# A fast-matrix-product encoder layer: first units of the second feed-forward product into the freed `h` buffers, gate rows three steps ahead of their dots

## The chip, the cores and the metric

The kernel runs on one core of one Trainium2 chip. The metric is the time of one launch on the device in microseconds, lower is better. Three runs of the kernel before gave 1226.02, 1227.35 and 1228.89 us, median 1227.35 us. All traces are from that single core.

## The reference, cut to what matters

One layer of a hybrid encoder: a token-mixing part (gated MLP beside windowed attention) and then a SwiGLU feed-forward part, each scaled by vectors that are computed from a condition `c`. Only the end of it is touched by the change:

```python
mod = jax.nn.silu(c) @ w_ada + b_ada
sh1, sc1, gt1, sh2, sc2, gt2 = jnp.split(mod[:, None, :], N_MOD, axis=-1)
...
h2 = rmsnorm(x, norm2_g) * (1.0 + sc2) + sh2
f_gate, f_up = jnp.split(h2 @ w_ffn_in, 2, axis=-1)
x = x + gt2 * ((jax.nn.silu(f_gate) * f_up) @ w_ffn_out)
```

There are 1024 tokens and 1024 channels, the hidden width is 2816, and all of it is float32. `gt2`, the gate vector, has 1024 entries, and each is the dot of `silu(c)` with a column of `w_ada`. The kernel holds everything transposed: channels on the 128 partitions, tokens along a row.

## The kernel before, in words

**Numbers.** Each float32 operand is split into a high part (a cast on ScalarE, ACT) and a low part (source minus high part, on VectorE, DVE). A product is then three matmuls of TensorE (PE): high by high, high by low, low by high. `wh`/`wl` and `oh`/`ol` are the high and low parts of weights or units; `raw` is what was loaded.

**The first product** (`h2 @ w_ffn_in`) runs over 22 tiles `f` of 128 hidden channels. A tile is done by a seven-product scheme in place of eight, so it has seven steps `i` = 0 to 6 (`STEPS`, L1512), each of 12 matmuls of 128x512. The blocks `B11` and `B21`, read by steps 0 and 1 alone, stand in the four buffers of the pool `hpool` with the tag `h`. For the tiles 2 to 5 steps 0 and 1 are done earlier, so these tiles have five steps here. After the step's `product(f, i)` comes `evict(f, i)`, which reads the bank of PSUM that the product wrote; step 6 accumulates into the bank that `evict(f, 4)` reads, so its matmuls wait for that read (`xs<-mm` on DVE).

**The hidden tiles** go to DRAM as they are finished (`hR`, and `hT` for the last two). The second product takes them as 4 by 2 blocks and `w_ffn_out` as 4 by 4 blocks and forms the block product by 26 products in place of 32 (the list `ORDER`, with eight more that are the plain tail of the last two hidden tiles). Each of the 26 products needs a linear combination of weight blocks (`a` values) and one of hidden blocks (`b` values). These combinations are made on DVE during the first product: the table `SUMS` gives for a step number s (counted from tile 2, step 2) which additions are done and which blocks are loaded, and into which of fifteen registers. A register is a 128x512 piece of a tile: registers 0 to 3 lie in one `sums` tile, 4 is `ss`, 5 and 6 are `t`, 7 to 10 are the other `sums` tile, `gt2["m"]`, and 11 to 14 are `hid`. A combination that a product needs is stored to the DRAM tensor `pU` by POOL's queue (`pool_dma`, L1396); loads go through SP's queue (`dma`, L1399), which issues in order and stops at the first transfer whose buffer isn't free.

**The gate vector.** `gt2_step(n)` (L2142) multiplies row n-1 of `w_ada` by the condition and sums it (the dot, `sums<-sums 128x1024` on DVE, in `ada_late`, L744), then issues the load of row n into the same half of `gt2["m"]`. The rows and the condition share the space of registers 7 to 10, which `SUMS` therefore uses only after the last dot.

**The second product** works on units: product p, group g of 128 in the contraction, a 128x768 float32 piece of `pU` (384 KB): 256 columns of an `a` value and 512 of a `b` value. A unit takes six matmuls. `fetch(n)` loads unit n, `split_step(n)` splits it, `after_unit(n)`, called after the matmuls of unit n, splits unit n+5 and fetches a later one. Units 0 to 2 are fetched during the last tile into `wpool`; the next ones, 3 to 11, after `ffn_ctx.close()`, into the pool `outp`, which lies in the space that the first product's `ffn` pool gives back. `load_acc` brings the residual rows (`mid<-x1d`, 512 KB each, eight of them, on POOL's queue), and `evict_out` adds a finished product to them. `tail_load` and `tail_split` bring and split the operands of the plain tail, whose split tiles also stand in `hpool`.

The order of the instructions on each engine is the order of the calls in the code.

Of the kernel before, what the change touches and what calls it, by code (L numbers as in the profile page):

```python
# [16 lines left out]
P = 128  # L17
# [223 lines left out]
def kernel(  # L241
# [1999 lines left out]
    raws, ready = {}, {}  # L2241
    outp = []

    def fetch(n):
        if n < len(work):
            p, g = work[n]
            if outp:
# [302 lines left out]
```

## Time and profile before

| | before |
|---|---|
| median of three runs | 1227.35 us |
| the profiled execution | 1226.68 us |
| span of that execution | 1224.9 us |
| mean granted TensorE clock | 0.995 |
| PE busy | 1201.7 us, 98% of the span |
| DVE busy | 1009.5 us, 82% |
| ACT busy | 610.3 us, 50% |
| mean rate of the DMA engines | 233 GB/s |

The profile is of one execution. A row of the timeline reads: start in us from the span's start, busy us, engine, line, operation, `out<-in`, shape, count, and in brackets the idle time just before with what ended it. A row of the chain of waits reads: start, us, what. A row of the busy times by stretch gives the stretch, its length and then busy time and count for PE, PEld (weight loads), DVE, ACT and POOL, the granted clock, the share of time that the DMA engines were busy, and GB/s. Between the span and the time of the execution lie 1.8 us.

### The profile page before, as it was taken

To read this page: it belongs to the slowest core of one execution; us is meant where nothing else is said; L and a number is where in the kernel's file an instruction comes from. 1 tells how busy PE (TensorE), PEld (TensorE's weight loads), DVE (VectorE), ACT (ScalarE), POOL (GpSimd) and SP (SyncE) were. 2 spreads that over 40 slices of the span, in tenths; PEclk is the share of its full clock that TensorE was granted. 3 is DMA by queue.
4 is the path that set the end of the run, shared out by engine and by line. 5 is a ranking of instruction groups with operands and counts; after the bars stand their busy time and mean duration, and the time that the engine had idled before them with its cause. 6 is when DMAs were issued, how large, how long until landed. Compare 5 with 4: busy or idle time off the path is not lost.

```text
span 1224.9 us, 16517 instructions
## 1 busy us (share of the span) xinstructions
PE 1201.7 (98%) x5593; PEld 997.6 (81%) x5593; DVE 1009.5 (82%) x1660; ACT 610.3 (50%) x1007; POOL 247.0 (20%) x342
## 2 busy tenths in 40 slices
PE   9999999999999999999997899999999998999998
PEld 7888888888888888888886688888888886788887
DVE  9999967889888876999876788888877866987895
ACT  6668844367856344736552233333333234754562
POOL 0124322104331100012001234333323322000001
PEclk9999999999999999999998999999999999999999
DMA  9745179653286633576227889888876749987884
GB/s 369 279 155 189 35 255 325 255 213 121 80 305 235 225 125 113 168 262 220 90 86 253 289 287 312 316 279 292 271 240 230 267 155 377 379 292 222 295 295 145
DMA packets 108166, 284.87 MB, mean 233 GB/s; under 512 B 13680, under 2 KB 24688, under 8 KB 107056
## 3 DMA queue, kind: packets, MB, share of 16 engines
q1 hardware_dynamic: 84576, 204.36, 49.6%
q0 software_dynamic: 23504, 79.45, 16.8%
q8 instruction: 44, 0.72, 0.2%
q14 instruction: 42, 0.34, 0.1%
HBM read 207.47 MB, written 76.28 MB: 232 GB/s over the span
## 4 chain that ended last, share of the span: by engine, by line
PE 82%; DVE 7%; DMA 6%; issue 2%; ACT 1%; POOL 0%; SPq 0%; DVEq 0%; ACTq 0%; POOLq 0%
PE mm L279 45%; PE at L279 37%; DMA raw<-pU 3%; DMA sums<-in_w_ada_dram 2%; DVE mid L279 1%; DVE wl L279 1%; DVE ws L279 1%; DMA raw<-in_w_tail_dram 1%; DVE sums L279 1%; ACT wh L279 1%; DVE hid L279 1%; DMA pU<-ss 1%; DVE lb L279 1%; DMA mid<-in_xA_dram 0%; DVE xs L279 0%
## 5 line engine op out<-in xcount | busy, mean ns | idle before, releaser
L279 PE MATMUL mm<-mid,wh 128*128 128x512 f32 x640 | 200.8, 395 | 11.0 <-DVE xs L279 10.5
L279 ACT CAST wh<-raw 128x1024 fp32r<-128x1024 f32 (+2 forms) x164 | 155.3, 949 | 86.5 <-PE mm L279 39.1
L279 DVE TENSOR_TENSOR wl<-raw,wh 128x1024 fp32r<-128x1024 f32 (+2 forms) x151 | 161.5, 1077 | 39.4 <-ACT wh L279 38.5
L279 PEld LDWEIGHTS mm<-mid,wh 128*128 128x128 f32 x640 | 121.3, 191 | 37.7 <-DVE xs L279 11.3
L279 PE MATMUL mm<-mid,wl 128*128 128x512 f32 x320 | 126.4, 395 | 0.1
L279 PE MATMUL mm<-wh,h 128*128 128x512 f32 x384 | 124.7, 397 | 0.2 <-ACT h L279 0.2
L279 PE MATMUL mm<-h,wh 128*128 128x512 f32 x304 | 94.4, 392 | 0.0
L279 PE MATMUL at<-h,wh 128*128 128x512 f32 x304 | 94.0, 391 | 0.0
L279 ACT CAST wh<-ws 128x1024 fp32r<-128x1024 f32 (+1 forms) x50 | 48.3, 966 | 76.5 <-DVE ws L279 75.1
L279 ACT CAST oh<-raw 128x768 fp32r<-128x768 f32 x73 | 60.8, 839 | 47.6 <-PE mm L279 20.8
L279 PEld LDWEIGHTS mm<-wh,h 128*128 128x128 f32 x384 | 70.8, 188 | 13.8 <-ACT h L279 0.4
L279 DVE TENSOR_TENSOR ol<-raw,oh 128x768 fp32r<-128x768 f32 x73 | 67.9, 953 | 15.4 <-ACT oh L279 15.1
L1397 POOL DMA_DIRECT2D pU<-sums x84 | 50.9, 607 | 111.0 <-DVE sums L279 104.7
L279 PEld LDWEIGHTS mm<-mid,wl 128*128 128x128 f32 x320 | 60.9, 190 | 13.8 <-DVE wl L279 1.0
L279 PE MATMUL mm<-wl,h 128*128 128x512 f32 x192 | 71.3, 392 | 0.0
L279 DVE TENSOR_TENSOR wl<-ws,wh 128x1024 fp32r<-128x1024 f32 (+1 forms) x50 | 55.9, 1118 | 15.8 <-ACT wh L279 15.7
L279 PEld LDWEIGHTS at<-h,wh 128*128 128x128 f32 x304 | 57.2, 189 | 11.8
L279 ACT ACTIVATE xs<-xs 128x512 f32<-128x512 f32 x21 | 13.3, 633 | 106.3 <-DVE xs L279 106.3
L279 PEld LDWEIGHTS mm<-h,wh 128*128 128x128 f32 x304 | 56.7, 188 | 11.6
L279 ACT ACTIVATE t<-t 128x512 f32<-128x512 f32 x46 | 28.4, 630 | 71.1 <-DVE t L279 71.1
L279 PE MATMUL mm<-h,wl 128*128 128x512 f32 x152 | 59.3, 390 | 0.0
L279 PE MATMUL at<-h,wl 128*128 128x512 f32 x152 | 59.3, 390 | 0.0
(360 smaller groups left out, 2999.7 us busy)
## 6 DMA issues: line engine op xcount, KB each, us to landing
raw<-pU SPq DMA_DIRECT2D x80, 384.0 KB, 5.0
pU<-sums POOLq DMA_DIRECT2D x71, 256.0 KB, 4.7
mid<-in_w_ada_dram SPq DMA_DIRECT2D x30, 512.0 KB, 8.1
raw<-in_w_gate_dram SPq DMA_DIRECT2D x26, 512.0 KB, 4.4
raw<-hR SPq DMA_DIRECT2D x40, 256.0 KB, 4.1
pU<-hid POOLq DMA_DIRECT2D x34, 256.0 KB, 4.3
raw<-in_w_ab_dram SPq DMA_DIRECT2D x16, 512.0 KB, 5.7
pd<-t POOLq DMA_DIRECT2D x24, 256.0 KB, 4.6
```

The source lines that it names most:

```text
L279: ins = f(*args, **kw)
L1397: nc.gpsimd.dma_start(dst, src)
```

## The change

Four things are altered, and all of them lie in the time from the first product's tile 2 to the start of the second product.

1. `gt2_step` runs at every third step (s = 0, 3, ... 24) in place of every second (s = 0, 2, ... 16).
2. The table `SUMS` is another one: the same 174 additions and 156 stores, with 113 loads in place of 106, in another order and with other registers. Registers 7 to 10 are used from s = 27 on; before it was from s = 18.
3. Units 3 to 9 are fetched during steps 2 to 5 of the last tile into `hpool`'s four `h` buffers, two units to a buffer. After `ffn_ctx.close()` units 10 to 18 are fetched in place of 3 to 11, and `after_unit(n)` fetches unit n+14, from n = 5 on, in place of n+12.
4. The tail operands and the residual rows are loaded at later units (`TAIL_AT`, `ACC_AT`).

```diff
 SUMS = (
-    (1, (), (('a', 0, 0, 0), ('a', 0, 4, 1))), (2, (), (('a', 0, 12, 2),)), (3, (), (('a', 0, 2, 3),)),
-    (4, (('a', 0, 16, 4, 0, 1, 1, -1),), ()), (5, (('a', 0, 25, 2, 1, 2, -1, -1),), (('a', 0, 10, 0),)),
-    (6, (('a', 0, 17, 4, 4, 3, 1, -1),), ()), (7, (('a', 0, 18, 1, 4, 1, 1, 1),), (('a', 0, 11, 2),)),
+    (1, (), (('a', 0, 4, 0), ('a', 0, 12, 1))), (2, (), (('a', 0, 0, 2),)), (3, (), (('a', 0, 2, 3),)),
+    (4, (('a', 0, 25, 4, 0, 1, -1, -1),), ()), (5, (('a', 0, 16, 2, 2, 0, 1, -1),), (('a', 0, 10, 1),)),
+    (6, (('a', 0, 17, 4, 2, 3, 1, -1),), ()), (7, (('a', 0, 18, 0, 4, 0, 1, 1),), (('a', 0, 11, 2),)),
...
+    first_raws = []
+
     def fetch(n):
         if n < len(work):
             p, g = work[n]
             if outp:
                 r = outp[0].tile([P, UCOL], F32, tag="raw2", name=nm("raw2"))
+            elif n < 3:
+                r = wpool.tile([P, UNIT], F32, tag="raw", name=nm("raw"))[:, :UCOL]
             else:
-                r = wpool.tile([P, UNIT], F32, tag="raw", name=nm("raw"))[:, :UCOL]
+                if n % 2:
+                    first_raws.append(hpool.tile([P, 2048], F32, tag="h", name=nm("first")))
+                r = first_raws[-1][:, (n + 1) % 2 * UNIT : (n + 1) % 2 * UNIT + UCOL]
...
     acc = {}
-    TAIL_AT = (11, 14, 17, 20)
-    ACC_AT = {4: 7, 8: 0, 14: 6, 18: 1, 24: 3, 45: 2}
+    FIRST_RAWS = 10
+    TAIL_AT = (18, 20, 22, 24)
+    ACC_AT = {13: 7, 17: 0, 23: 6, 27: 1, 31: 3, 55: 2}
...
-                if s < 18 and s % 2 == 0:
-                    gt2_step(s // 2)
+                if s < 27 and s % 3 == 0:
+                    gt2_step(s // 3)
                 run_sums(s)
+            if f == NF - 1 and 2 <= i < 6:
+                for n in (2 * i - 1, 2 * i):
+                    if n < FIRST_RAWS:
+                        fetch(n)
...
-        for n in range(3, 12):
+        for n in range(FIRST_RAWS, FIRST_RAWS + 9):
             fetch(n)
...
             split_step(n + AHEAD_OF)
-            fetch(n + 12)
+            if n + AHEAD_OF + 9 >= FIRST_RAWS + 9:
+                fetch(n + AHEAD_OF + 9)
```

An entry of `SUMS` is (s, additions, loads). An addition is (kind, group or pair of groups, value, register written, two registers read, two signs); a load is (kind, group, value, register).

DVE around the first two dots, from tile 2's step 5 on. `sums_6249,acc_mod` is the dot, `xs_6242<-at` is `evict(2, 5)`, `hid` is `evict(2, 6)`, `ss_6251` is register 4, and the names in brackets are the semaphores waited for (DMAHW for loads, DMASW for stores by POOL). Before:

```order
L279 SCALAR_TENSOR_TENSOR sums_6249,acc_mod<-sums_6249 128x1024 [waits DMAHW7_49,DMAHW0_49]
L279 TENSOR_TENSOR xs_6242<-at_6254,xs_6242 128x512 [waits PE_49]
L279 TENSOR_TENSOR ws_5754<-raw_6161,ru 128x512 [waits DVE_49]
L279 TENSOR_TENSOR ws_5754<-raw_6161,ws_5754 128x512
L279 SCALAR_TENSOR_TENSOR hid_6063<-xs_6267,xs_6242 128x512 [waits DMASW4_49,Activation_49]
L279 SCALAR_TENSOR_TENSOR hid_6063<-mm_5854,t_1093_5870 128x512 [waits DMASW3_49,PE_49]
L279 TENSOR_TENSOR wl_6323<-ws_5754,wh_6322 128x1024 [waits Activation_49]
L279 SCALAR_TENSOR_TENSOR sums_6249,acc_mod<-sums_6249 128x1024 [waits DMAHW3_49]
L279 TENSOR_TENSOR ss_6251<-sums_6250 128x512 [waits DMAHW2_49,DMAHW1_49]
L279 TENSOR_TENSOR wl_6351<-ru,wh_6350 128x512 [waits Activation_49]
L279 SCALAR_TENSOR_TENSOR sums_6250<-sums_6250 128x512 [waits DMAHW4_49]
L279 SCALAR_TENSOR_TENSOR sums_6249,acc_mod<-sums_6249 128x1024 [waits DMAHW7_49]
```

And now:

```order
L283 TENSOR_TENSOR xs_6242<-at_6254,xs_6242 128x512 [waits PE_49]
L283 SCALAR_TENSOR_TENSOR sums_6249,acc_mod<-sums_6249 128x1024 [waits DMAHW7_49,DMAHW0_49]
L283 TENSOR_TENSOR ws_5754<-raw_6161,ru 128x512 [waits DVE_49]
L283 TENSOR_TENSOR ws_5754<-raw_6161,ws_5754 128x512
L283 SCALAR_TENSOR_TENSOR hid_6063<-xs_6267,xs_6242 128x512 [waits DMASW4_49,Activation_49]
L283 SCALAR_TENSOR_TENSOR hid_6063<-mm_5854,t_1093_5870 128x512 [waits DMASW3_49,PE_49]
L283 TENSOR_TENSOR wl_6323<-ws_5754,wh_6322 128x1024 [waits Activation_49]
L283 SCALAR_TENSOR_TENSOR ss_6251<-sums_6250 128x512 [waits DMAHW2_49,DMAHW1_49]
L283 TENSOR_TENSOR wl_6349<-ru,wh_6348 128x512 [waits Activation_49]
L283 TENSOR_TENSOR sums_6250<-sums_6250 128x512 [waits DMAHW3_49]
L283 SCALAR_TENSOR_TENSOR sums_6249,acc_mod<-sums_6249 128x1024 [waits DMAHW4_49]
L283 TENSOR_TENSOR ss_6251<-sums_6250 128x512 [waits DMAHW5_49,DMASW1_49,DVE_49]
```

The first dot now stands behind `xs` instead of ahead of it, and where there were two dots behind the first there is one. Behind that dot, now as before, stands the addition that writes `ss` a second time and waits for the store of its first contents.

SP's queue at the seam of the two products, from the last load into `raw` (unit 2) on. Before:

```order
L1400 DMA raw_8950<-pU 128x768 [waits DMAHW5_49,DVE_49,Activation_49]
L1400 DMA raw_1422_9054<-pU 128x768 [waits DMAHW1_49,DMAHW6_49,DVE_49,PE_49]
L1400 DMA raw_1423_9056<-pU 128x768 [waits DMAHW7_49]
L1400 DMA raw_1424_9058<-pU 128x768 [waits DMAHW0_49]
L1400 DMA raw_1425_9060<-pU 128x768
```

And now:

```order
L1404 DMA raw_8957<-pU 128x768 [waits DMAHW4_49,DVE_49,Activation_49]
L1404 DMA first_8982<-pU 128x768 [waits DMAHW5_49,PE_49]
L1404 DMA first_8982<-pU 128x768 [waits DMAHW6_49,DMASW7_49]
L1404 DMA first_9003<-pU 128x768 [waits DMAHW7_49,PE_49]
L1404 DMA first_9003<-pU 128x768 [waits DMAHW0_49]
L1404 DMA first_9025<-pU 128x768 [waits DMAHW1_49,PE_49]
L1404 DMA first_9025<-pU 128x768 [waits DMAHW2_49]
L1404 DMA first_9042<-pU 128x768 [waits DMAHW3_49,DMASW6_49,PE_49]
L1404 DMA raw_1426_9072<-pU 128x768 [waits DMAHW4_49,DVE_49,PE_49]
L1404 DMA raw_1427_9074<-pU 128x768 [waits DMAHW5_49]
```

`raw_14..` are the buffers of `outp`, whose first load waits for the last product that reads the `ffn` pool (PE); `first` are the seven units in `hpool`, which wait for the products that read `B11` and `B21`.

212 rows, old and new, of the table SUMS are left out of this document.

## The prediction

> **What bounds the kernel now.** TensorE does, but for two holes. I read the busy times by stretch first, cut at the seams of the part that is edited (the columns are named in the first row):
>
> ```profile
> core 0: us, PE busy (x) PEld busy (x) DVE busy (x) ACT busy (x) POOL busy (x), PEclk, DMA share, GB/s
> 651.10:708.20 57.10, 46.14 (x182) 36.13 (x181) 43.78 (x68) 13.60 (x20) 12.65 (x19) 0.91 0.77 263
> 727.20:746.30 19.10, 19.10 (x86) 15.84 (x85) 17.02 (x26) 6.49 (x9) 7.63 (x14) 1.00 0.91 309
> 1013.20:1022.50 9.30, 9.25 (x40) 6.94 (x39) 6.56 (x9) 4.17 (x5) 5.36 (x8) 1.00 1.02 386
> 1022.50:1037.00 14.50, 10.89 (x40) 6.82 (x39) 7.06 (x8) 5.50 (x7) 0.00 (x0) 1.00 1.03 397
> 1037.00:1073.20 36.20, 34.35 (x148) 27.16 (x147) 34.51 (x41) 26.74 (x33) 0.00 (x0) 1.00 1.03 382
> 1073.20:1217.80 144.60, 144.60 (x639) 119.83 (x638) 114.36 (x138) 73.98 (x88) 7.61 (x14) 1.00 0.78 257
> ```
>
> From 1073 on PE is never idle, so nothing can be won there. The holes are 651 to 708 (tiles 3 to 5 of the first product) and 1013 to 1073 (the start of the second). What a hole costs follows from the matmuls in it, since a lowered clock after a stall counts too:
>
> ```profile
> 651.09 0.39 PE L279 MATMUL mm<-b22h,wh 128*128 128x512 f32 x1
> 1013.22 0.39 PE L279 MATMUL mm<-wh 128*128 128x512 f32 x1
> 1073.01 0.39 PE L279 MATMUL at<-wh 128*128 128x512 f32 x1
> ...
> 708.21 38.18 PE at L279 x168
> 746.39 2.72 PE mm L279 x12
> ```
>
> At full pace a step of 12 takes 2.72 us, a matmul 0.2267. From 651.09 to 708.21 are 15 steps: 57.12 against 40.8, so **16.3 us** are lost. From 1013.22 to 1073.01 stand units 0 to 34 and one tail product, 35 x 6 + 12 = 222 matmuls: 59.8 against 50.3, so **9.5 us** are lost. With both holes closed the execution of 1226.68 would take 1200.9.
>
> The waits of the first hole, from DVE's groups by shape (busy, mean ns, then idle before) and from the timelines:
>
> ```profile
> L279 DVE SCALAR_TENSOR_TENSOR sums<-sums 128x1024 f32<-128x1024 f32 x8 | 9.8, 1221 | 14.5 <-DMA sums<-in_w_ada_dram 14.5
> ...
> 651.72 1.23 DVE L279 SCALAR_TENSOR_TENSOR sums<-sums 128x1024 f32<-128x1024 f32 x1 [3.98 <-DMA sums<-in_w_ada_dram]
> 652.87 0.69 DVE L279 TENSOR_TENSOR xs<-at,xs 128x512 f32<-128x512 f32 x1
> 657.10 1.22 DVE L279 SCALAR_TENSOR_TENSOR sums<-sums 128x1024 f32<-128x1024 f32 x1
> 658.24 0.69 DVE L279 TENSOR_TENSOR ss<-sums 128x512 f32<-128x512 f32 x1
> 658.84 0.68 DVE L279 TENSOR_TENSOR wl<-ru,wh 128x512 fp32r<-128x512 f32 x1
> 659.45 0.69 DVE L279 SCALAR_TENSOR_TENSOR sums<-sums 128x512 f32<-128x512 f32 x1
> 664.65 1.22 DVE L279 SCALAR_TENSOR_TENSOR sums<-sums 128x1024 f32<-128x1024 f32 x1 [4.52 <-DMA sums<-in_w_ada_dram]
> 666.81 0.69 DVE L279 TENSOR_TENSOR ss<-ss,sums 128x512 f32<-128x512 f32 x1 [0.92 <-DVE sums L279]
> 668.74 0.68 DVE L279 TENSOR_TENSOR xs<-mm,xs 128x512 f32<-128x512 f32 x1
> ...
> 669.48 1.22 PE L279 MATMUL mm<-mid,wh 128*128 128x512 f32 x2 [6.92 <-DVE xs L279]
> 703.67 0.73 PE L279 MATMUL mm<-mid,wh 128*128 128x512 f32 x2 [3.53 <-DVE xs L279]
> ```
>
> All of DVE's 14.5 us before dots is waiting for gate rows. The chain shows how long a row takes and what a stall does to the clock, the queue when rows are issued, and POOL when `ss` is stored:
>
> ```profile
> 644.38 7.32 DMA sums<-in_w_ada_dram
> ...
> 659.22 6.67 DMA pU<-ss
> ...
> 680.39 7.73 DMA sums<-in_w_ada_dram
> ...
> 703.67 4.54 PE mm L279 x12
> ...
> 652.98 0.33 SPq L1400 DMA_DIRECT2D sums<-in_w_ada_dram  x1
> 658.35 0.33 SPq L1400 DMA_DIRECT2D sums<-in_w_ada_dram  x1
> ```
>
> Two steps are 5.44 us; rows take up to 7.7. A dot that waits holds up `evict(f, 4)`, and PE, whose step 6 needs it, stops. The 12 matmuls after the 3.53 us of idling take 4.54 in place of 2.72: 1.8 us more.
>
> **Part by part.** *Gate rows.* Three steps are 8.16 us, above the longest row. The first row has nothing ahead of it: it still lands at 651.70, so the first dot starts at 651.72 as before. From there I add start-to-start times of the rows above in the new order: dot 1.15; two `ws`, two `hid` and the `wl` up to 657.10, which the old order puts between 653.47 (after `xs`) and 657.10, 3.63; `ss` 0.60; `wl` 0.61; `sums` 0.6. The second dot is reached at 658.3; its row, issued at 652.98 as before, was used without a wait at 657.10. So the 4.5 us wait is gone. The other dots have at most the 7.7 us row against 8.16. I cost all later dots at 0; their cover is the 0.4 us between.
>
> *What is late next* is the second `ss`, reached at 658.3 + 1.15 = 659.5. It overwrites the register that the first `ss` (now at 651.72 + 1.15 + 3.63 = 656.5) has still to store. Queued behind it stand two `ws` and `xs`, for which PE waits from 662.4. Before, `xs` ended 2.6 us after that addition started (666.81 to 669.42). Without a wait it ends at 662.1: loss 0. If, as before, 8.57 us pass between the two `ss` (658.24 to 666.81), the second starts at 665.1, `xs` ends at 667.7, PE idles 5.3 and, as after 3.53, pays 1.8 for the clock: 7.1. Now no gate row is queued in front of the store, so I take the page's median for such stores:
>
> ```profile
> pU<-sums POOLq DMA_DIRECT2D x71, 256.0 KB, 4.7
> ...
> 708.20:1013.20 305.00, 304.88 (x1345) 252.29 (x1344) 245.01 (x366) 104.63 (x145) 101.89 (x177) 1.00 0.78 265
> ```
>
> Issued 1.0 after its addition (658.24, then 659.22) it lands at 662.2; `xs` ends at 664.8, PE idles 2.4. For the clock I take 0.6, nearer to the short idling below than to 3.53. **Loss left: 3.0, bounds 0 and 7.1.**
>
> The Trainium skill ("TensorE: Matmul & The Clock Gate", Part 1, the HAM clock gate) says that the clock halves only after an idle window of about 3.4 us. The rows agree on 3.53; by that rule 2.4 us of idling costs no clock and the sum is 0.6 lower. The skill's "DMA: Bandwidth & Descriptors" (Anatomy of one DMA) fits 2.0 us plus bytes/436 GB/s, by which a 512 KB row lands in an estimated 3.2 us and two steps would do: a rule against this change. The rows say 7.3 and 7.7 where the dots waited, and they decide; by the rule the store too would land early and the sum be some 2.7 lower.
>
> *Is there DMA rate for the shorter time?* 651 to 708 moved 57.1 x 263 GB/s = 15.0 MB. Three of its eight 512 KB rows leave it: 13.4 MB in 40.8 + 3 us are 306 GB/s. Tile 7 ran at 309 with PE full (second stretch above). So it fits, without much room.
>
> *The new table* does as many additions with seven loads more, 1.8 MB at some 309 GB/s or 6 us of DMA time over 350 us. More of its additions overwrite a register two steps after it was written and stored: 22 in place of 12, four of them in a tile's step 3, ahead of `evict(f, 4)`. At the 8.57 us above against 5.44 each of these could wait 3.1 us: 12.5 at worst. At the median it is 1.0 + 4.7 against 5.44: nothing. Between 708 and 1013 PE idled 0.12 us with the old table. **I take 1.0, bounds 0 and 12.5**, near the lower since the median row is.
>
> *First units.* The second hole is a queue of transfers:
>
> ```profile
> 1018.95 17.45 DMA raw<-pU
> ...
> 1022.51 0.83 ACT L279 CAST wh<-raw 128x768 fp32r<-128x768 f32 x1 [1.43 <-DMA raw<-pU]
> 1036.50 0.84 ACT L279 CAST oh<-raw 128x768 fp32r<-128x768 f32 x1 [1.49 <-DMA raw<-pU]
> 1037.39 2.80 ACT L279 CAST wh<-raw 128x768 fp32r<-128x768 f32 x3
> ...
> 1016.38 2.14 POOL L1397 DMA_DIRECT2D mid<-x1d  x3
> 1032.13 0.47 PE L279 MATMUL mm<-oh 128*128 128x512 f32 x1 [1.64 <-DVE mid L279]
> 993.80:1012.80 19.00, 19.00 (x86) 15.74 (x85) 14.10 (x21) 7.00 (x10) 7.22 (x13) 1.00 0.53 183
> 999.56 12.42 SPq L1400 DMA_DIRECT2D raw<-pU  x4
> ```
>
> Casts of units 7 (1022.51) to 13 (1036.50) start 2.33 us apart because residual rows on POOL's queue share the engines; PE eats a unit in 1.36. (After the 1.64 us of idling matmuls kept their pace, the short case meant above.) Now units 3 to 9 follow unit 2 (SP's first issue at 999.56), into buffers free after step 1 of the last tile, two steps before. Seven of 0.39 MB at the 386 of the fill take 7 us; the DMA engines there are busy 0.53 of the time. They are in by about 1011, and unit 3 is multiplied at 1013.22 + 4.08 = 1017.3. Units 10 to 18 then take the places in the queue that 3 to 11 had: unit 10 + k lands when 3 + k did. Unit 18 takes unit 11's place, 1022.51 + 4 x 2.33 = 1031.8, and, with 1.9 for cast and low part, needed at 1013.2 + 18 x 1.36 - 1.9 = 1035.8; unit 20 at 1036.5 against 1038.5; then casts follow each other (three in 2.80). Least margin 2.0, so a loss of 0 by arrivals. DVE is the other end: from 1013 to 1073 it does 6.56 + 7.06 + 34.51 = 48.1 us of work, now in 50.3, so tail splits and evictions may push PE now and then. **Loss left 0.8, bounds 0 and 3** (two stops like the 1.64). The later tail and residual loads are costed at 0: POOL's loads depend on no unit, and the tail is used from unit 35 on.
>
> Sum for the profiled execution: 1226.68 - 16.3 - 9.5 + 3.0 + 1.0 + 0.8 = 1205.7. The median of the runs is 0.7 above it, so the forecast is **1206.4 us**.
>
> **The rivals.** *The store takes the row's place* (chance 0.15): the 7.1 and some 4 of the table's 12.5 are paid, 1206.4 + 4.1 + 3.0 = 1213.5. For it: 6.67 for that very store; against it: five rows in place of eight beside it. *The seam stays starved* (0.12): `first` loads stand in order behind unit 2's, which waits for a free buffer, and POOL's eight residual loads are untouched; if half of the 9.5 stays, 1206.4 + 4 = 1210.4; two thirds with a worse store, 1215. Against it: margins of 2 us and more. *Nothing is gained* (0.02): dots merely wait elsewhere and the seam moves to units 10 on: 1227. *Slower* (0.03): two-step overwrites stop PE through tiles 6 to 19. With 19 of the 22 there it takes over 1.3 us each to pay back 24 us; at 1.5 us it is 1206.4 + 19 x 1.5 - 1 = 1234. Against it: ten such places there cost 0.12 us before. **The forecast** itself has 0.68, with 1201 (all hidden) to 1211.
>
> The range is 1201 to 1215: from both holes shut to the second rival's worse end. About 0.2% is what a measurement here tells from no change, 2.5 us. Faster by more: 0.68 + 0.15 + 0.12 = 0.95; within 0.02; slower 0.03.
>
> **What would show it.** Right: no DVE idling before dots except the first; PE's idling before `mm<-mid` in tile 3 at 1 to 4 us with the second `ss` behind `pU<-ss`; units 3 to 9 cast with no wait for `raw<-pU`; 1073.01's counterpart 50 to 52 us after the second product's start. Wrong: PE waits in tiles 7 to 19, or casts of units 10 to 20 that still come 2.33 us apart with PE idle.

## The result and the profile after

The changed kernel takes 1215.11 us (median of four runs, 1214.80 to 1216.48); beside it the kernel before took 1227.85 (1226.02 to 1228.89). The ratio is 0.990, with an interval of 0.9883 to 0.9917: 12.7 us faster. The forecast was 1206.4, and its range ended at 1215, so the direction was right and the size was not: of the 21 us that were to come, 12.7 came. The profiled execution took 1215.11, its span is 1213.3.

First the busy times of the changed kernel by stretch, cut where the prediction cut the kernel before (tiles 3 to 5, the rest of the first product, the start of the second in three pieces, the remainder):

```profile
core 0: us, PE busy (x) PEld busy (x) DVE busy (x) ACT busy (x) POOL busy (x), PEclk, DMA share, GB/s
651.00:699.30 48.30, 44.00 (x187) 35.94 (x186) 38.19 (x57) 13.23 (x19) 12.63 (x19) 0.96 0.87 299
699.30:1007.90 308.60, 306.06 (x1343) 251.27 (x1343) 249.69 (x375) 103.73 (x145) 101.88 (x177) 1.00 0.79 276
1007.90:1016.00 8.10, 8.10 (x38) 6.70 (x37) 7.97 (x11) 7.17 (x11) 3.82 (x6) 1.00 1.03 408
1016.00:1034.00 18.00, 17.85 (x79) 14.47 (x78) 12.72 (x16) 7.53 (x10) 1.53 (x3) 1.00 1.03 395
1034.00:1061.20 27.20, 26.32 (x112) 20.28 (x111) 24.78 (x30) 19.71 (x25) 0.00 (x0) 1.00 1.04 386
```

The first hole has shrunk and is still there (4.3 us without work), the second is nearly shut, and there is a third place that the kernel before hardly had: 2.5 us without work between 699 and 1008, where it had 0.12 (from 708 to 1013). DVE's group of dots and the transfers that touch `ss` say what has become of the first hole:

```profile
L283 DVE SCALAR_TENSOR_TENSOR sums<-sums 128x1024 f32<-128x1024 f32 x8 | 9.8, 1219 | 3.5 <-DMA sums<-in_w_ada_dram 3.5
```

```profile
L1401 POOL DMA_DIRECT2D pU<-ss x2: 707/716/725, 658.8 to 666.0; - x2
...
DMA to landing us min/median/max: 2.5/3.0/6.1
```

The dots wait 3.5 us in place of 14.5, as meant, 2.56 of it for the first row. The first store of `ss` is issued at 658.8 and takes 6.1 us to land. The timelines of DVE, TensorE and ScalarE, in order of time:

```profile
652.32 0.39 PE L283 MATMUL mm<-b22h,wh 128*128 128x512 f32 x1
653.05 1.23 DVE L283 SCALAR_TENSOR_TENSOR sums<-sums 128x1024 f32<-128x1024 f32 x1 [2.56 <-DMA sums<-in_w_ada_dram]
657.83 0.68 DVE L283 SCALAR_TENSOR_TENSOR ss<-sums 128x512 f32<-128x512 f32 x1
659.64 1.22 DVE L283 SCALAR_TENSOR_TENSOR sums<-sums 128x1024 f32<-128x1024 f32 x1
664.98 0.69 DVE L283 TENSOR_TENSOR ss<-sums 128x512 f32<-128x512 f32 x1 [4.12 <-issue]
666.92 0.68 DVE L283 TENSOR_TENSOR xs<-mm,xs 128x512 f32<-128x512 f32 x1
667.66 0.73 PE L283 MATMUL mm<-mid,wh 128*128 128x512 f32 x2 [4.30 <-DVE xs L283]
...
713.92 0.39 PE L283 MATMUL at<-tt2h,wh 128*128 128x512 f32 x1
...
759.07 0.69 DVE L283 TENSOR_TENSOR t<-sums,t 128x512 f32<-128x512 f32 x1 [2.45 <-DMA pU<-t]
...
1008.43 0.39 PE L283 MATMUL mm<-wh 128*128 128x512 f32 x1
...
1009.19 3.04 ACT L283 CAST oh<-first 128x768 fp32r<-128x768 f32 x4
1012.13 2.30 ACT L283 CAST wh<-first 128x768 fp32r<-128x768 f32 x3
1014.33 0.83 ACT L283 CAST oh<-raw 128x768 fp32r<-128x768 f32 x1
...
1022.31 0.84 ACT L283 CAST wh<-raw 128x768 fp32r<-128x768 f32 x1 [1.49 <-DMA raw<-pU]
1024.65 0.84 ACT L283 CAST wh<-raw 128x768 fp32r<-128x768 f32 x1 [1.50 <-DMA raw<-pU]
...
1031.57 1.73 ACT L283 CAST oh<-raw 128x768 fp32r<-128x768 f32 x2 [1.41 <-DMA raw<-pU]
...
1061.40 0.39 PE L283 MATMUL at<-wh 128*128 128x512 f32 x1
```

The second dot (659.64) waits for nothing. The addition behind it, the second that goes to `ss`, stands 4.12 us under `<-issue`, a wait that the profile can't name; the store's 658.8 + 6.1 = 664.9 names it. TensorE stops for 4.30 us. At 759.07 an addition waits 2.45 us for a store outright. At the seam units 3 to 9 (`first`) are cast without a wait, and units 12 to 18 still come 2.33 us apart.

The rows of TensorE at 652.32, 713.92, 1008.43 and 1061.40 are marks, each the same matmul as in the kernel before, which has the second one here:

```profile
721.75 0.39 PE L279 MATMUL at<-tt2h,wh 128*128 128x512 f32 x1
```

Between the marks lie 240, 1284 and 222 matmuls, at full pace 54.4, 291.0 and 50.3 us. What a stretch takes beyond that is its loss. Worked out in the same way for every kernel that ran:

| kernel | median us | ratio to before (interval) | lost, tile 3 to step 4 of tile 6 | lost, step 5 of tile 6 to tile 21 | lost, seam |
|---|---|---|---|---|---|
| before | 1227.85 | 1 | 16.3 | 0.4 | 9.5 |
| the change | 1215.11 | 0.9900 (0.9883 to 0.9917) | 7.2 | 3.5 | 2.6 |
| e1_table | 1228.39 | 1.0001 (0.9991 to 1.0011) | 15.8 | 1.7 | 9.7 |
| e2_gates_table | 1223.55 | 0.9956 (0.9939 to 0.9973) | 10.3 | 3.0 | 9.4 |
| e3_seam | 1221.38 | 0.9944 (0.9925 to 0.9963) | 14.6 | 1.6 | 2.7 |
| e4_ss_reg | 1210.91 | 0.9858 (0.9835 to 0.9880) | 3.2 | 2.4 | 2.7 |
| e5_recol | 1208.77 | 0.9837 (0.9821 to 0.9854) | 4.9 | 0.3 | 2.9 |
| e6_tail | 1208.83 | 0.9846 (0.9827 to 0.9864) | 2.9 | 0.7 | 3.3 |
| e7_acc_sp | 1205.04 | 0.9811 (0.9794 to 0.9827) | 4.7 | 0.0 | 0.0 |
| e8_all | 1205.67 | 0.9818 (0.9798 to 0.9837) | 4.0 | 0.3 | 0.0 |
| e9_gates | 1207.45 | 0.9838 (0.9823 to 0.9853) | 5.2 | 0.9 | 0.0 |
| e10_gates_load | 1207.93 | 0.9840 (0.9825 to 0.9855) | 7.2 | 0.1 | 0.0 |
| e11_two_steps | 1216.01 | 0.9908 (0.9891 to 0.9925) | 14.6 | 0.0 | 0.0 |

The losses are of one execution each. Stretches with the same code show their scatter: tiles 3 to 6 lost 7.2 and 10.3 (the change and e2), and 2.9 to 4.9 (e5 to e8). The first mark itself lies between 650.9 and 652.3, and these differences are there long before the first edited step (1500 matmuls earlier 319.6 in the change against 318.4 before). e1 to e4, e5 to e8 and e9 to e11 ran on three different chips, each group beside the kernel before, so kernels of different groups are best compared by their ratios.

### The profile page after: what moved, and what is told of

The parts are those of the page before. It is cut to its first block, busy times and chain, and to the rows that moved or that the text cites. A ratio compares the mean times of both kernels' runs of the same rounds, so it can differ in the third digit from the quotient of the medians.

```text
span 1213.3 us, 16539 instructions
## 1 busy us (share of the span) xinstructions
PE 1198.4 (99%) x5593; PEld 995.7 (82%) x5593; DVE 1009.2 (83%) x1660; ACT 608.9 (50%) x1007; POOL 247.0 (20%) x342
## 4 chain that ended last, share of the span: by engine, by line
PE 80%; DMA 6%; DVE 6%; issue 4%; POOL 2%; ACT 1%; SPq 0%; POOLq 0%; DVEq 0%; ACTq 0%
PE mm L283 46%; PE at L283 34%; DMA raw<-pU 2%; DMA pU<-sums 1%; DVE wl L283 1%; DVE ws L283 1%; POOL pU L1401 1%; DMA raw<-in_w_q_dram 1%; DVE mid L283 1%; DMA mid<-in_w_ada_dram 1%; DMA sums<-in_w_ada_dram 1%; DVE sums L283 1%; DMA pU<-t 1%; DVE hs L283 0%; POOL hR L1401 0%
## 5 line engine op out<-in xcount | busy, mean ns | idle before, releaser
L283 DVE TENSOR_TENSOR wl<-raw,wh 128x1024 fp32r<-128x1024 f32 (+2 forms) x148 | 158.7, 1080 | 37.3 <-ACT wh L283 36.4
L283 ACT CAST oh<-raw 128x768 fp32r<-128x768 f32 x69 | 57.5, 839 | 43.4 <-PE mm L283 22.3
L283 DVE TENSOR_TENSOR ol<-raw,oh 128x768 fp32r<-128x768 f32 x69 | 64.2, 954 | 11.5 <-ACT oh L283 10.8
L283 ACT ACTIVATE t<-t 128x512 f32<-128x512 f32 x46 | 28.4, 630 | 71.2 <-DVE t L283 71.2
```

Source lines behind the costliest of these rows:

```text
L283: ins = f(*args, **kw)
```

## The experiments

### The parts apart

**e1_table** is the kernel before with the new table alone; gates and seam stay.

```diff
 SUMS = (
-    (1, (), (('a', 0, 0, 0), ('a', 0, 4, 1))), (2, (), (('a', 0, 12, 2),)), (3, (), (('a', 0, 2, 3),)),
+    (1, (), (('a', 0, 4, 0), ('a', 0, 12, 1))), (2, (), (('a', 0, 0, 2),)), (3, (), (('a', 0, 2, 3),)),
...
```

> The kernel before with the new table of additions alone; gate rows stay two steps ahead and the second product's first units stay where they were. Reading of the two traces (parts add up): tiles 3 to 5 lose what they lost before, since dots still wait for their rows, and tiles 6 to 13 give back the 3.5 us that the aligned TensorE records show there (the difference to before shrinks from 8.66 us at 699.35 to 5.3 at the second product's start): 1227.9 + 3.5 = 1231, with TensorE idle in tiles 8 to 11 where the changed kernel has it (1.27 at 770.11). Rival A, the 3.5 us come from the gate rows that now run on into tile 6, and not from the table: 1228, no idling in tiles 8 to 11. Rival B, the prediction's term of 1.0: 1229.

Measured 1228.39, ratio 1.0001 (0.9991 to 1.0011): 1231 is excluded, and so is any cost over 1.4 us. The trace of this run loses 1.7 us from the end of tile 6 on, about what e3 loses there with the old table (1.6). In the kernels that have the new table and the later gate rows, the loss is 3.5 (the change), 3.0 (e2) and, with one register moved, 2.4 (e4). So the 3.5 us aren't a fixed price of the table. Whether its short distances cost more once gate rows run on into tile 6, or the executions merely differ, these runs don't tell apart; what the stops wait for is shown by e5 below.

**e2_gates_table** is the change without its third and fourth parts, **e3_seam** these two alone:

```diff
-                if s < 27 and s % 3 == 0:
-                    gt2_step(s // 3)
+                if s < 18 and s % 2 == 0:
+                    gt2_step(s // 2)
```

(the lines of e3 against the change; its table is the old one too)

> The changed kernel without its third part: gate rows three steps ahead and the new table, but the second product's first units loaded as before. Parts add up: 1227.9 - 9.7 + 3.5 = 1221.7. The prediction's own terms (16.3 - 3.0 - 1.0 = 12.3 gained): 1215.6. Rival, the two holes are not separate: the seam is starved by what the first product leaves behind in the queues, so that its loss moves with the gates: anything under 1219.

> The kernel before with the third part alone: units 3 to 9 of the second product loaded into the hidden buffers during the last tile, with the later tail and residual loads; gates and table as before. Parts add up: 1227.9 - 6.7 = 1221.2. The prediction's term (9.5 - 0.8 = 8.7 gained): 1219.2. Rival, the loads in the last tile cost something there too, or the table's last additions and these loads get in each other's way only in the changed kernel: 1219 or less here with the old table.

e2 gained 0.44% (5.4 us of the 1228.56 that the kernel before took beside it), e3 0.56% (6.9): together 12.3 against the change's 12.7. The parts add up within their intervals, and the seam's loss is the same with either (9.4 to 9.7 with the old seam, 2.6 and 2.7 with the new). The prediction's own terms, 1215.6 and 1219.2, fall.

### The store that holds `ss`

**e4_ss_reg** changes the register of one addition:

```diff
-    (6, (('a', 0, 17, 4, 2, 3, 1, -1),), ()), (7, (('a', 0, 18, 0, 4, 0, 1, 1),), (('a', 0, 11, 2),)),
+    (6, (('a', 0, 17, 5, 2, 3, 1, -1),), ()), (7, (('a', 0, 18, 0, 5, 0, 1, 1),), (('a', 0, 11, 2),)),
...
-                elif s == 12:
-                    regs.update({5: tmp(), 6: tmp()})
```

(the `regs.update` line moves to step 0)

> The changed kernel with one register moved: registers 5 and 6 exist from the first step on, and the second addition that went to ss (the 4.30 us stop at 667.66) goes to register 5, so it overwrites nothing that is still being stored. Nothing else moves; the row loaded into ss at step 8 stays. Theory, the store's landing (6.09 us after its issue) holds that addition: the stop and the slow matmuls behind it go, 4.3 + 1.0 us: 1215.1 - 5.3 = 1209.8. Rival A, the addition waits for something else (a gate row or a transfer that the trace does not name): 1215. Rival B, the stop moves to the next thing that is late there, since all transfers of this stage are late: 1212 to 1214, with another DVE wait of 2 us or more before 700.

Measured 1210.91, ratio 0.9858: 4.2 us under the change by the medians, 5.2 by the ratios. Its timeline, the same place:

```profile
657.13 0.69 DVE L283 SCALAR_TENSOR_TENSOR ss<-sums 128x512 f32<-128x512 f32 x1
...
660.08 0.69 DVE L283 TENSOR_TENSOR t<-sums 128x512 f32<-128x512 f32 x1
...
662.01 0.68 DVE L283 TENSOR_TENSOR xs<-mm,xs 128x512 f32<-128x512 f32 x1
...
662.75 0.73 PE L283 MATMUL mm<-mid,wh 128*128 128x512 f32 x2 [0.19 <-DVE xs L283]
```

The addition, now to `t`, follows its dot at once; 4.30 us of idling have become 0.19. Nothing but its target has changed (and the step at which registers 5 and 6 are set up), so the landing of `ss` was the wait.

**e5_recol** gives all additions and loads other registers. Operations, order, steps and addresses stay:

```diff
-    (39, (('a', 1, 17, 11, 8, 2, 1, -1), ('b', 0, 22, 6, 9, 6, 1, 1)), (('a', 1, 10, 13),)),
+    (39, (('a', 1, 17, 4, 3, 2, 1, -1), ('b', 0, 22, 10, 11, 8, 1, 1)), (('a', 1, 10, 12),)),
```

(one line of the table; its second addition is the one at 759.07 above, which overwrote `t`, register 6, two steps after it was stored)

> The changed kernel with the same additions, loads and stores in the same steps, but other registers for them, chosen so that as little as possible is overwritten while it is still being stored: additions that overwrite a register stored two steps before go from 22 to 1, loads that do so from 28 to 7 (registers 5 and 6 exist from the first step on). Theory, stores that have not landed hold both the second ss addition and the additions in tiles 6 to 13: with the 4.9 us that moving the one register gained, the 3.5 us of tiles 6 to 13 go too: 1210.9 - 3.5 = 1207.4, and TensorE stands still nowhere over 0.5 us between 708 and 1003. Rival A, in tiles 6 to 13 values that are loaded again come late, or all transfers do: 1210 to 1211, with additions waiting for loads. Rival B, loads that hold SP's queue matter too (gate rows and weights behind them): 1206 or less.

Measured 1208.77, ratio 0.9837. Busy times by stretch:

```profile
700.20:704.20 4.00, 3.96 (x10) 2.85 (x11) 3.44 (x6) 1.04 (x1) 1.66 (x3) 0.60 0.64 213
...
708.00:1003.40 295.40, 295.35 (x1303) 244.23 (x1302) 241.66 (x361) 101.64 (x142) 100.06 (x174) 1.00 0.80 283
```

From 708 to 1003 TensorE is without work for 0.05 us in place of 2.5: what stopped it in tiles 6 to 13 was the overwriting of registers whose stores had not landed, and not late values (rival A). Between 708 and 1000 DVE's additions wait 12.7 us for such stores in the changed kernel and 0.9 here. All seven kernels with these registers lose 0.0 to 0.9 us in that stretch, the six others 0.4 to 3.5. The run changes additions that overwrite (22 to 1) and loads that do (28 to 7) together, so it does not say what share the loads have. The time is 2.1 us under e4 by the medians, 2.6 by the ratios; e4 lost 2.4 us there where this run loses 0.3. That is less than the 3.5 expected from the changed kernel's execution, and a stop at 700 has grown besides, which the first row is about (last section).

### The residual rows at the seam

While units 10 to 18 come 2.33 us apart, these transfers run in the changed kernel (issues from 1002 to 1035, KB each, median us to landing):

```profile
raw<-pU SPq DMA_DIRECT2D x19, 384.0 KB, 12.6
mid<-x1d POOLq DMA_DIRECT2D x8, 512.0 KB, 9.6
```

384 + 512 KB at the 395 GB/s of the window above are 2.32 us: each unit of SP's queue lands with one residual row of POOL's. `ACC_AT` names units for six of these rows, but on POOL nothing holds them to that: all eight are issued between 1005.38 and 1017.5. **e6_tail** moves the tail's loads, **e7_acc_sp** these six rows, **e8_all** both, each on top of e5:

```diff
-    TAIL_AT = (18, 20, 22, 24)
+    TAIL_AT = (14, 16, 18, 24)
+    SPLIT_AT = (24, 26, 28, 30)
...
-                load_acc(ACC_AT[n])
+                load_acc(ACC_AT[n], dma)
```

(the first part is e6, the second, with `load_acc` issuing on the queue it is given, is e7)

> As the run with other registers, and the tail's first three loads issued four units earlier (after units 14, 16 and 18), its splits where they were. In the changed kernel the tail's second load landed at 1046.84, DVE stood idle 2.03 us at 1047.95 for the split behind it, and TensorE then 0.68 us at 1050.85. Theory, the late tail load is what is left of the seam's loss: about 1 us less than the run with other registers. Rival, DVE has no time to spare in this stage (48.1 us of work in 50.3), so that the stop only moves: the same time within 0.4 us. Rival B, the earlier tail loads delay units 19 on: up to 1 us more.

> As the run with other registers, and six of the eight residual-row loads on SP's queue, in the order in which the program names them, in place of POOL's, where all eight are issued at once because nothing holds them. Theory, the residual rows are why units 10 to 18 arrive 2.33 us apart: they now arrive about 1.0 to 1.2 us apart, and the stops of TensorE by arrivals go: 0.3 to 1 us less than the run with other registers. Rival, with seven units in hand the spacing no longer matters: units 10 to 18 come closer together and the time is the same within 0.4 us.

> Other registers, earlier tail loads and residual rows on SP's queue together. If the two seam edits act on different stops: 1 to 2 us less than the run with other registers, 1205.5 to 1206.5. If DVE bounds the seam: the same within 0.5 us.

e6: 1208.83 against 1208.77 of e5, nothing, and the seam's loss is no smaller (3.3 against 2.9). The stop has moved to the fourth split:

```profile
1051.05 1.23 DVE L297 TENSOR_TENSOR tail<-raw,tail 128x1024 fp32r<-128x1024 f32 x1 [2.82 <-ACT tail L297]
```

e7: 1205.04, 3.7 us under e5, and the seam has no loss left. Its busy times by stretch, and ScalarE's timeline:

```profile
1001.20:1012.00 10.80, 10.80 (x49) 8.94 (x48) 10.80 (x15) 9.07 (x12) 1.11 (x2) 1.00 1.03 408
1012.00:1030.00 18.00, 18.00 (x81) 14.91 (x80) 17.12 (x22) 11.09 (x14) 0.00 (x0) 1.00 1.01 370
1030.00:1051.60 21.60, 21.60 (x97) 17.88 (x96) 17.43 (x20) 14.37 (x18) 0.00 (x0) 1.00 1.03 378
```

```profile
1010.43 1.72 ACT L297 CAST oh<-raw 128x768 fp32r<-128x768 f32 x2 [1.05 <-DMA raw<-pU]
1012.43 0.84 ACT L297 CAST wh<-raw 128x768 fp32r<-128x768 f32 x1 [0.28 <-PE at L297]
1013.79 0.84 ACT L297 CAST wh<-raw 128x768 fp32r<-128x768 f32 x1 [0.52 <-PE at L297]
```

From 1012.43 on casts come 1.36 us apart, at TensorE's own pace, and wait for TensorE; the last to wait for `raw<-pU` is the one at 1010.43. So the rival falls, the spacing did matter. e6's theory falls too: the tail was late because the queue was crowded. Its first load is issued 28.4 us after the second product's start in e7 (1029.78) and 33.0 after it in the changed kernel (1041.45). With the rows out of the way the tail edit is worth nothing (e8, 1205.67). e7 puts the rows on another queue and by that also later (five of the six are issued from 1021.10 to 1052.21); it does not tell the one from the other. It is the best version that ran, 0.83% under the change by the medians, 0.90% by the ratios.

### What is left of the first hole

e7's one stop over 0.6 us stands at 697.9. DVE's timeline there:

```profile
693.92 1.23 DVE L297 SCALAR_TENSOR_TENSOR sums<-sums 128x1024 f32<-128x1024 f32 x1 [2.33 <-DMA sums<-in_w_ada_dram]
...
696.65 0.69 DVE L297 TENSOR_TENSOR sums<-sums,t 128x512 f32<-128x512 f32 x1 [1.50 <-DMA t<-in_w_blk_dram]
```

The first is the seventh dot, the second an addition of the same step. **e9_gates** puts the last three dots a step later, **e10_gates_load** also loads that `t` a step earlier:

```diff
+GATES_AT = (0, 3, 6, 9, 12, 15, 19, 22, 25)
...
-                if s < 27 and s % 3 == 0:
-                    gt2_step(s // 3)
+                if s in GATES_AT:
+                    gt2_step(GATES_AT.index(s))
```

> As the run with other registers and residual rows on SP's queue (1205.0), whose one stop of TensorE over 0.6 us behind the first product's start is at 697.89 (2.24 us, and half the clock for the 4 us behind it, 3.7 us in all). There the dot of the seventh row waited 2.33 us for its row, and the addition behind it 1.50 us for a value from the block weights. Here the last three dots come later: after steps 19, 22 and 25 in place of 18, 21 and 24. Theory A, the row is the cause: the stop goes, 1201.3. Theory B, the row and the value were issued together, and the addition alone would wait as long: the stop stays as it is, 1204.5 to 1205.5.

> As the run with the last three dots later, and the load of that value (row 3 of the block weights) one step earlier, after step 14 in place of 15, into the same register. Theory A: the same as the run with the dots alone, 1201.3. Theory B, both were late: only now the stop goes, 1201 to 1202. Rival, all transfers of this stretch are late because the engines are full (322 GB/s in the 7.8 us ahead of the stop): the stop moves to another dot or addition, 1203.5 to 1205.

e9, 1207.45, is slower than e7 (0.9838 against 0.9811, with intervals that barely overlap). The addition, now without a dot ahead of it, waits until about the same moment:

```profile
697.51 0.69 DVE L298 TENSOR_TENSOR sums<-sums,t 128x512 f32<-128x512 f32 x1 [5.22 <-DMA t<-in_w_blk_dram]
```

So theory A falls, and theory B has the mechanism but not the time: the moved dots brought a stop of their own (2.19 us between two matmuls at 706.9, which e7 doesn't have). In e10, 1207.93, with the same new stop, the addition waits 4.9 us for its other value, loaded from the block weights as well. Its rival comes nearest, though its time (1203.5 to 1205) is missed: values from the block weights are late whichever is moved ahead. Spreading the transfers of this stretch further was not tried, so what closes these 3 to 5 us stays open.

**e11_two_steps** asks the reverse: e7 with the old gate steps.

> As the run with other registers and residual rows on SP's queue (1205.0), but with the gate rows two steps ahead of their dots again, as in the kernel before. Theory, the rows are what dots wait for, whatever the registers: the dots' waits come back (14.5 us of DVE before) and tiles 3 to 5 lose 12 to 16 us in place of 4.6: 1213 to 1217. Rival, stores that had not landed were the larger part of that hole before too: 1206 to 1209.

Measured 1216.01, 11 us over e7 by the medians, 12 by the ratios. DVE's group of dots:

```profile
L297 DVE SCALAR_TENSOR_TENSOR sums<-sums 128x1024 f32<-128x1024 f32 x8 | 9.8, 1221 | 13.2 <-DMA sums<-in_w_ada_dram 13.2
```

The dots wait 13.2 us again, and tiles 3 to 6 lose 14.6. The gate part is worth 11 us where nothing takes the place of its wait.

## Why the prediction was wrong, step by step

The reading of the kernel before held: two holes, one of dots that wait for gate rows (e11), one of units that wait for their turn in the queues (e7). The second dot runs without a wait, as worked out, and the next thing late is the second `ss`, as named. Both signs that the prediction named for being wrong are there as well: TensorE stops in the tiles behind 6 (the longest is 1.27 us at 770.11), and units 12 to 18 are cast 2.33 us apart. What failed are sizes, and at the seam a wait for arrivals that was put at nothing. The sum stood at 1205.7 for the profiled execution; 1215.11 is 9.4 more. Of that 4.2 are the gate term, 2.0 the table's, 1.9 the seam's, and 1.2 lie ahead of the first mark (652.32 against 651.09), in code that no edit touches, within the scatter of that mark.

**Gate region, 3.0 taken, 7.2 measured (bounds 0 and 7.1).** The step that failed is "no gate row is queued in front of the store, so I take the page's median". The median of such stores stands for the whole span; this one took 6.1 us. The very same store before took 7.5, and the 6.67 that the prediction read off the chain stops short of its landing:

```profile
L1397 POOL DMA_DIRECT2D pU<-ss x2: 707/716/725, 659.2 to 667.8; - x2
...
DMA to landing us min/median/max: 3.9/5.7/7.5
```

(the first of the two is the 7.5: 659.2 + 7.5 = 666.7, and the second `ss` started at 666.81). No gate row was left in front of the store, but the stretch holds as many weights as before in less time: it moves 299 GB/s in place of 263. That this rate is what kept the store so long was not tested by a run of its own. With the store at 6.1 in place of 4.7, and issued 1.0 after its addition, TensorE idled 4.30 in place of 2.4. The clock was put at 0.6; the 12 matmuls behind the stop lost about 1.7. Most of the other 1.2 is a stop at 711, behind a dot and an addition that waited 0.9 and 1.0 us for their loads: the 0.4 us between the longest row and three steps was too little cover for "all later dots at 0". The rival that gave the upper bound (the store takes the row's place, with 7.1 and 4 of the table) is what happened, and it had 0.15. That its 7.1 is so near the 7.2 is partly luck: it was made of 5.3 of idling and 1.8 for the clock, without the stop at 711.

**Table, 1.0 taken, 3.0 more than before measured.** The mechanism was named (additions that overwrite what was stored two steps earlier, 22 in place of 12), and e5 shows that it is the right one. The size rested again on the median, 1.0 + 4.7 against 5.44, "nothing". But 5.7 against 5.44 leaves no room at all, and a stop comes from the late end of a spread, not from its middle: the two `ss` stores alone took 2.5 and 6.1. And "ten such places there cost 0.12 us before" was one execution: the same table lost 1.6 in e3.

**Seam, 0.8 taken, 2.6 measured (bounds 0 and 3).** Arrivals were put at 0 and cost 0.8: unit 21, due at 1008.43 + 21 x 1.36 = 1037.0, starts at 1037.75. That seven units are "in by about 1011" was too early, relative to the product's start. Unit 18 was to land 18.6 us after that start (1031.8 against 1013.2) and was cast 23.1 after it (1031.57 against 1008.43); with the 1.9 us for cast and low part that is 25.0, and it is needed 18 x 1.36 = 24.5 after. The margin was gone. Counting seven units at 386 GB/s as 7 us left out the stores and the first two residual rows that run beside them: unit 10 is cast 5.9 us after the start (1014.33), and from unit 12 on each unit brings a residual row with it. The rows were costed at 0 with the words "POOL's loads depend on no unit". That is right, and it is the reason for the loss: not held to any unit, all eight go out within 12 us (e7).

The 0.8 that was taken stood for tail splits and evictions on DVE. TensorE's waits for these, all behind unit 21, cost the larger part, 1.9. The longest stop there:

```profile
1047.95 1.23 DVE L283 TENSOR_TENSOR tail<-raw,tail 128x1024 fp32r<-128x1024 f32 x1 [2.03 <-ACT tail L283]
1050.85 0.47 PE L283 MATMUL mm<-wh 128*128 128x512 f32 x1 [0.68 <-DVE mid L283]
```

The split waits until the tail's load has landed and been cast, the eviction `mid<-mm` stands behind it on DVE, and TensorE waits for the eviction. That "the tail is used from unit 35 on" was no cover, because its splits stand on DVE among the work for units 30 and later. With the rows out of the way this loss is gone too (e7).

The clock rule from the Trainium skill's "TensorE: Matmul & The Clock Gate" (Part 1, the HAM clock gate), by which it takes an idle window of about 3.4 us to halve the clock, does not hold for all stops here: 2.05 us were enough in e5 and 1.80 in e10 (last section). By it the sum would have been 0.6 lower, further off. The fit from the Trainium skill's "DMA: Bandwidth & Descriptors" (Anatomy of one DMA), which the page gives for the gpsimd path, that of the store, would have had the store land early and the sum 2.7 lower. The row of 6.1 us decides against it under this load.

## What to carry to other kernels

When a wait is taken away, look at the next instruction in line that needs a transfer, and price it with the landing that this very transfer had in this stretch; the median over the span is no bound for a stop. An addition into a register that is still being stored waits for the store's landing: choosing registers by the distance from store to overwriting cost no instruction here and took 2 to 3 us of such stops away. A load that waits for nothing goes out early, whatever unit the program names for it: the residual rows all left by 1017.5. To hold it back, put it on the queue behind the work that it shall follow.

## What the runs showed of the hardware

TensorE's clock fell after a stop of 2.05 us in e5 and stayed at about half for 4 us:

```profile
697.77 0.39 PE L297 MATMUL at<-h,wl 128*128 128x512 f32 x1
700.21 0.50 PE L297 MATMUL at<-b22h,wh 128*128 128x512 f32 x1 [2.05 <-ACT t L297]
```

The stretch from 700.20 to 704.20, shown above, has a granted clock of 0.60 and 10 matmuls where full pace would have 17.6. In e8 the same stop was 1.25 us, and the next 4 us ran at full clock:

```profile
698.70:700.40 1.70, 0.45 (x3) 0.03 (x2) 1.70 (x3) 1.53 (x2) 0.21 (x1) 1.00 0.67 246
700.40:704.40 4.00, 3.96 (x16) 2.98 (x17) 3.43 (x6) 1.05 (x1) 1.64 (x3) 1.00 0.65 212
```

Counted from one matmul's start to the next, less one at full pace, and with the matmuls lost to the clock, the stop of 2.05 us cost about 4 and that of 1.25 about 1.4. Length alone does not decide. e9 and e10 both have a stop of 1.80 us at the same place (before 709.08 and 709.38), and these are the 4 us behind each, e9 first:

```profile
709.10:713.10 4.00, 4.00 (x18) 3.32 (x19) 2.67 (x6) 1.89 (x3) 1.12 (x2) 1.00 0.86 273
709.40:713.40 4.00, 4.00 (x12) 3.15 (x13) 1.77 (x4) 1.88 (x3) 1.11 (x2) 0.63 0.85 273
```

After the one the clock stayed full, after the other 6 of 18 matmuls were lost. What else decides, these runs don't show. Nor does the price grow with the stop: after the 4.30 us of the changed kernel about as much was lost to the clock (1.7) as after the 2.05.

The landing of transfers of one size varied widely: the two 256 KB stores of `ss` in the changed kernel, 7 us apart (658.8 and 666.0), took 6.1 and 2.5 us. The busy times while each was under way:

```profile
658.80:664.90 6.10, 4.56 (x21) 3.43 (x19) 2.06 (x4) 0.00 (x0) 1.45 (x2) 1.00 0.94 336
666.00:668.50 2.50, 0.84 (x3) 0.73 (x4) 1.95 (x4) 1.05 (x1) 0.68 (x1) 0.96 0.59 194
```

The slow one ran while the engines moved 336 GB/s, the quick one while they moved 194.
